# One dense tile's gates from one-hots, two tiles' gates added into a zeroed array, selection per head

## The chip, the cores and the metric

The kernel runs on one core of one Trainium2 chip. The metric is device time in microseconds, the median of several runs. TensorE (PE) does the matmuls, VectorE (DVE) the elementwise work, the top-16 and the selection, ScalarE (ACT) copies, gelu and exponentials and issues some DMAs, GpSimd (POOL) a few elementwise operations and all indirect DMAs, and SyncE (SP) issues the plain loads. PEld is TensorE's loading of weights, which overlaps its matmuls.

## What is computed

A decoder trunk of two layers over 512 tokens and 16 meta tokens, width 1024. Layer 0 mixes tokens by pooling, layer 1 by a stick-breaking attention; after each comes a PEER block, an expert layer of 128 x 128 = 16384 experts, which is where nearly all of the time goes:

```python
def chunk(hx):                                            # h: (tokens, 1024)
    q = einsum('btd,dq->btq', hx, w_query)                # 8 heads x 2 halves x 128
    s = einsum('bthpc,hpnc->bthpn', q, sub_keys)          # 128 keys for each half
    top_s, top_i = lax.top_k(s, 16)
    cand_s = top_s[..., 0, :, None] + top_s[..., 1, None, :]
    cand_i = top_i[..., 0, :, None] * 128 + top_i[..., 1, None, :]
    best_s, best_pos = lax.top_k(cand_s, 16)              # of the 256 sums
    expert = take_along_axis(cand_i, best_pos)
    gate = softmax(best_s)
    act = gelu(einsum('btd,bthkd->bthk', hx, u[expert]))
    return einsum('bthk,bthkd->btd', gate * act, v[expert])
```

So every token takes 8 x 16 = 128 experts, each with a gate.

## The kernel before

The 512 tokens are four tiles of 128. PEER treats them in two ways. Tile 3 (`GATHERED`) and the meta tokens are gathered: for each of the 128 slots of a token, POOL fetches that expert's 8 KB row of u and v by an indirect DMA (L343, 128 rows at once, one for each partition), DVE forms the dot product with the token (L355), ACT the gelu, and DVE adds the gated v half to the output (L367). A row is four quarter-steps of `row_step()`: fetch, dot, gelu, add. Tiles 0 to 2 are dense: all 16384 experts are computed for their 384 tokens. The experts come as 128 blocks j of 128. A u step (`u_parts`, L307) loads the block's u, splits it in a high and a low part (`w_hi` on ACT, L279; `w_lo` = `w` - `w_hi`, L281 on DVE or L283 on POOL), does 24 matmuls into `psu` (L314), a gelu on ACT and writes the activation `ac` to DRAM (`aout`). A v step (`v_step`, L660) loads v (L663), the activations (L668) and, for each four blocks, the gates (`gt`, L672), splits v (`v_hi` on ACT, `v_lo` on DVE, L676), multiplies activations by gates (`wt`, L678), splits that (`wt_hi` on ACT, L682; `wt_lo` on DVE, L683) and does 18 matmuls into six PSUM banks `y` (L690), which gather over all 128 blocks.

The gates of the dense tiles, zero for all but 128 of a token's 16384 experts, are made by one-hots (`build_gates`, L553): for four tokens at a time DVE makes three one-hot tiles `ab`, PE multiplies them (8 matmuls into `pg`, L574 and L576, one block), ACT evacuates that to `stage` (L581) and sends a stage of 32 tokens to the DRAM array `gout` (L584). That is 32 blocks a tile, 96 a layer.

A layer's PEER block runs in three stages:

- Stage A: for each of 8 heads, two query projections (weights split as those of u), scores, and on DVE the top-16 of both halves of all four tiles (`top16`, L391). For the gathered tile the selection (`select`, L399: 80 candidate sums, their top-16, the look-up of the experts' two indices by one-hots at L439 to L445, the softmax) follows per head, and its rows are queued. u steps are put between as a plan says: `WQ_DVE` and `WQ_PE` are its costs of a head in us, a u step is put in while PE's sum lies below DVE's. Here `w_lo` is made on POOL.
- Stage B: per dense tile one selection over all 8 heads (128 slots a partition), then its 32 gate blocks. `gate_stream` yields a cost at each step and quarters of u steps are put between by it; rows are worked off at a pace of `ROW_PERIOD`. The order on PE is kept as written (`pin`), `w_lo` is made on DVE.
- Stage C: the u steps that are left alternate with v steps, then v steps alone; rows go on at their pace. Nothing of the next layer starts before its end.

All indirect DMAs are on POOL's queue q0. Loads of w, v, `ac` and `gt` are issued by SP, in the order written, and `aout` and `gout` writes by ACT. Layer 0's PEER is preceded by the pool mixer (0 to 55 us), layer 1's by the attention (1399 to 1795 us).

## Time and profile before

| | |
|---|---|
| Median of 3 runs | 3134.08 us (3131.5 to 3134.3) |
| The profiled execution | 3127.99 us, its span 3126.3 us |
| Mean granted PE clock | 0.984 of 2.4 GHz |
| PE, PEld busy | 2999.0 us (96%), 2671.7 us (85%) |
| DVE, ACT, POOL busy | 2449.1 us (78%), 1354.3 us (43%), 688.7 us (22%) |
| DMA moved | 758.52 MB, 243 GB/s on the mean |

Busy is the time in which an engine had an instruction running. A matmul's end is modelled, so several can overlap in the records, and prices of PE are best read from one start to another. The span is cut by hand into stages; layer 0's A, B and C begin at 55.5, 264 and 650.4 us, layer 1's at 1795, 2010 and 2391.3 us. DMA share is the mean busy share of 16 DMA engines; a packet is one piece of a transfer, by one descriptor.

### The profile page before, as it was taken

Reading aid. Unit: us, or ns where it says so; the run is one execution under the profiler, and the core shown is the slowest. Engines: PE = TensorE matmul, PEld = TensorE weight load, DVE = VectorE, ACT = ScalarE, POOL = GpSimd, SP = SyncE. Lnnn points to the kernel's source line nnn. Section 1 sums busy time; section 2 is a strip of 40 time slices with the busy share of each in tenths; the row PEclk is TensorE's granted clock in tenths of the full one; section 3 lists DMA queues with packets and bytes.
Section 4 is the critical chain, followed back from the end, with each engine's and each line's share of the span. In section 5 each row is a group of like instructions: output and inputs, shape, how many; then the busy total and the mean of one; then the engine's idle time right before and its main releaser. Section 6 shows DMA issues by size and latency. Waiting matters only on the chain.

```text
span 3126.3 us, 45813 instructions
## 1 busy us (share of the span) xinstructions
PE 2999.0 (96%) x16514; PEld 2671.7 (85%) x16514; DVE 2449.1 (78%) x5636; ACT 1354.3 (43%) x2184; POOL 688.7 (22%) x704
## 2 busy tenths in 40 slices
PE   8988999999999999999999989799999999999999
PEld 7887988988888888879965778798898888888887
DVE  3999998878777778786456469999987777777765
ACT  3443645643333333335455334354655333333333
POOL 3431311111111111114245244222110111111100
PEclk9999999999999999999999999999999999999999
DMA  3435877799989899762100344477878998989875
GB/s 134 179 121 202 282 265 265 274 360 329 338 312 321 314 329 329 273 245 90 55 1 1 108 177 144 158 262 269 303 253 326 358 314 321 331 308 333 307 250 164
DMA packets 286708, 758.52 MB, mean 243 GB/s; under 512 B 23184, under 2 KB 176784, under 8 KB 248336
## 3 DMA queue, kind: packets, MB, share of 16 engines
q1 hardware_dynamic: 222544, 390.92, 36.8%
q0 software_dynamic: 39168, 285.23, 24.9%
q10 hardware_dynamic: 24768, 79.44, 6.6%
q8 instruction: 129, 2.11, 0.3%
q14 instruction: 99, 0.81, 0.1%
HBM read 673.99 MB, written 81.53 MB: 242 GB/s over the span
## 4 chain that ended last, share of the span: by engine, by line
PE 77%; DVE 16%; DMA 3%; ACT 2%; issue 1%; POOL 0%; SPq 0%; DVEq 0%; ACTq 0%; POOLq 0%
PE y L690 31%; PE psu L314 27%; PE pg L574 3%; PE pg L576 3%; PE pp L124 2%; PE pp L125 2%; PE pp L123 2%; DVE mr L395 1%; DVE prod L355 1%; DVE w_lo L281 1%; DMA gt<-gout 1%; DVE ti L397 1%; DVE hx L367 1%; DMA w<-in_peer_ut_dram 1%; DVE ti L394 1%
## 5 line engine op out<-in xcount | busy, mean ns | idle before, releaser
L343 POOL DMA_INDIRECT row<-in_peer_uv_dram,ei x272 | 383.3, 1409 | 1833.1 <-DVE hx L367 1481.9
L314 PE MATMUL psu<-n_hi,w_lo 128*128 128x384 f32 x2048 | 701.5, 343 | 42.4 <-DVE w_lo L281 39.9
L314 PE MATMUL psu<-n_hi,w_hi 128*128 128x384 f32 x2048 | 720.4, 352 | 11.5 <-ACT ac L321 7.2
L314 PE MATMUL psu<-n_lo,w_hi 128*128 128x384 f32 x2048 | 703.0, 343 | 0.6 <-DVE n_lo L118 0.6
L279 ACT ACTIVATE w_hi<-w 128x1024 fp32r<-128x1024 f32 x288 | 305.6, 1062 | 467.7 <-PE psu L314 373.2
L690 PE MATMUL y<-v_lo,wt_hi 128*128 128x512 f32 x1536 | 473.6, 390 | 1.6 <-DVE v_lo L676 1.6
L690 PE MATMUL y<-v_hi,wt_hi 128*128 128x512 f32 x1536 | 473.8, 390 | 0.5 <-ACT v_hi L675 0.5
L690 PE MATMUL y<-v_hi,wt_lo 128*128 128x512 f32 x1536 | 473.6, 389 | 0.0
L314 PEld LDWEIGHTS psu<-n_hi,w_lo 128*128 128x128 f32 x2048 | 394.0, 192 | 49.0 <-DVE w_lo L281 45.8
L314 PEld LDWEIGHTS psu<-n_hi,w_hi 128*128 128x128 f32 x2048 | 395.4, 193 | 17.8 <-ACT ac L321 7.5
L314 PEld LDWEIGHTS psu<-n_lo,w_hi 128*128 128x128 f32 x2048 | 394.0, 192 | 5.5 <-DVE n_lo L118 1.1
L682 ACT ACTIVATE wt_hi<-wt 128x384 fp32r<-128x384 f32 x256 | 134.3, 525 | 574.0 <-PE y L690 295.5
L683 DVE TENSOR_TENSOR wt_lo<-wt,wt_hi 128x384 fp32r<-128x384 f32 x256 | 142.5, 557 | 264.3 <-ACT wt_hi L682 264.3
L281 DVE TENSOR_TENSOR w_lo<-w,w_hi 128x1024 fp32r<-128x1024 f32 x228 | 278.2, 1221 | 83.2 <-ACT w_hi L279 82.6
L690 PEld LDWEIGHTS y<-v_lo,wt_hi 128*128 128x128 f32 x1536 | 288.1, 188 | 63.3 <-DVE v_lo L676 2.9
L690 PEld LDWEIGHTS y<-v_hi,wt_lo 128*128 128x128 f32 x1536 | 288.3, 188 | 60.4
L355 DVE SCALAR_TENSOR_TENSOR prod<-row,hnat 128x1024 bf16<-128x1024 f32 x272 | 337.7, 1241 | 0.6 <-DMA row<-in_peer_uv_dram,ei 0.5
L367 DVE SCALAR_TENSOR_TENSOR hx<-row,gwt,hx 128x1024 f32<-128x1024 f32 x256 | 334.5, 1307 | 2.1
L690 PEld LDWEIGHTS y<-v_hi,wt_hi 128*128 128x128 f32 x1536 | 286.8, 188 | 52.8 <-ACT v_hi L675 0.9
L676 DVE TENSOR_TENSOR v_lo<-v,v_hi 128x1024 fp32r<-128x1024 f32 x256 | 312.2, 1219 | 5.4 <-ACT v_hi L675 5.2
L581 ACT ACTIVATE stage<-pg 128x512 f32<-128x512 f32 x192 | 216.9, 1137 | 149.2 <-PE pg L576 146.3
L675 ACT ACTIVATE v_hi<-v 128x1024 fp32r<-128x1024 f32 x256 | 270.8, 1058 | 10.6 <-DMA v<-in_peer_uv_dram 9.5
(313 smaller groups left out, 4695.0 us busy)
## 6 DMA issues: line engine op xcount, KB each, us to landing
w<-in_peer_ut_dram SPq DMA_DIRECT2D x256, 512.0 KB, 5.9
v<-in_peer_uv_dram SPq DMA_DIRECT2D x256, 512.0 KB, 6.1
gout<-stage ACTq DMA_DIRECT2D x24, 2048.0 KB, 8.4
gt<-gout SPq DMA_DIRECT2D x64, 768.0 KB, 10.2
aout<-ac ACTq DMA_DIRECT2D x148, 192.0 KB, 4.0
ac<-aout SPq DMA_DIRECT2D x148, 192.0 KB, 5.9
w<-in_peer_wq_dram SPq DMA_DIRECT2D x32, 512.0 KB, 3.4
wn<-in_w_kv_dram SPq DMA_DIRECT2D x8, 1024.0 KB, 5.5
```

The lines of the kernel that those rows point to most:

```text
L279: amark.append(sc.activation(whi, w, AF.Copy))
L281: vmark.append(v.tensor_sub(wlo, w, whi.bitcast(F32)))
L314: m = pin(pe.matmul(ps[:, :ND], a[:, k, :], b[:, k, c0:c0 + ND], start=st, stop=en))
L343: gp.indirect_dma_start(out=row, out_offset=None, in_=peer_uv, in_offset=bass.IndirectOffsetOnAxis(ap=item[1], axis=0))
L355: v.scalar_tensor_tensor(prod, row[:, :D], 1.0, hn_nat[i], ALU.mult, ALU.mult, accum_out=dot)
L367: v.scalar_tensor_tensor(acc, row[:, D:], wt, acc, ALU.mult, ALU.add)
L581: sc.activation(stage[:, :, o:o + TG].rearrange("p j t -> p t j"), pg, AF.Copy, scale=1.0 / GSCALE)
L675: amark.append(sc.activation(vhi, v32, AF.Copy))
L676: vmark.append(v.tensor_sub(vlo, v32, vhi.bitcast(F32)))
L682: sc.activation(whi, wt, AF.Copy)
L683: vmark.append(v.tensor_sub(wlo, wt, whi.bitcast(F32)))
L690: pe.matmul(y[n][half], wp[:, ts], vq[:, half * 512:(half + 1) * 512], start=st, stop=en)
```

## The change

Gates. Only tile 0's gates are still built from one-hots (`BUILT` = 1: 32 blocks a layer), in an array of their own, `gbuilt`. For tiles 1 and 2 the array `gout` is cleared, and each gate is added to its element there: `gates_out` works out the element's index for each slot, and `scatter` issues an indirect DMA with an addition for one slot of 128 tokens, 4 bytes for each partition, 2 tiles x 16 slots x 8 heads = 256 a layer. Each waits for the same tile's scatters of the head before (or for the clearing): two heads of a token may choose the same expert. The clearing is four DMAs a layer on ACT's queue from a zero tile, for layer 0 within the pool mixer, for layer 1 at the start of attention.

Selection. `select` runs once a head over all four tiles (64 slots a partition, 16 for each tile) in stage A, for the dense tiles too; stage B has none.

Pace. `w_lo` is always made on DVE. With `WQ_DVE` 33 and `WQ_PE` 15.5 / 14.5 the plan puts 38 u steps (layer 0) and 40 (layer 1) into stage A. There each head issues 17 scatters and eight quarter-steps of rows (two rows). Stage B runs u steps up to `EARLY` = 118, one gate block beside each of the first u steps, the scatters left spread evenly over them, and rows at `ROW_PERIOD`. PE's order is no longer pinned. In stage C ten u steps are left beside 128 v steps. `gt` is read in two parts; the second waits for the last head's scatters.

```diff
+BUILT = 1
...
-ROW_PERIOD = ((18.0, 13.5), (18.0, 13.5))
-WQ_DVE = (19.0, 19.0)
-WQ_PE = (15.5, 12.5)
+ROW_PERIOD = (12.0, 13.5)
+ROWS_A = 2
+WQ_DVE = 33.0
+WQ_PE = (15.5, 14.5)
 GATHERED = (3,)
 LEAD = (2, 2)
-QUIET = 16
+EARLY = 118
+SCATTER_A = 17
...
+    zero = const([P, 512], F32, "zero")
+    gp.memset(zero, 0.0)
...
+    NB = P // TB
+    NS = nd - BUILT
+    gbuilt = [dram.tile([P, BUILT * NB, NK, TB], F32, name=f"gbuilt{layer}") for layer in range(2)]
+    gouts = [dram.tile([P * NS * NB * NK * TB, 1], F32, name=f"gout{layer}") for layer in range(2)]
+    cleared = [[], []]
+    def clear_gates(layer, part, parts):
+        g = gouts[layer].rearrange("(p c f) o -> p c (f o)", p=P, f=512)
+        n = NK * NS * P // 512 // parts
+        cleared[layer].append(sc.dma_start(g[:, part * n:(part + 1) * n, :],
+                                           zero.unsqueeze(1).to_broadcast([P, n, 512])))
...
             pre(0)
+            clear_gates(0, 0, 4)
             fold()
             for i in range(1, NT):
                 pre(i)
+                clear_gates(0, i, 4)
...
-                if gating[0]:
-                    vmark.append(v.tensor_sub(wlo, w, whi.bitcast(F32)))
-                else:
-                    gp.tensor_sub(wlo, w, whi.bitcast(F32))
+                vmark.append(v.tensor_sub(wlo, w, whi.bitcast(F32)))
...
+            to_scatter = []
+            placed = {}
+            issued = []
+            def gates_out(h, i1, i2, gate):
+                ds = slice(BUILT * TK, nd * TK)
+                ef = gr.tile([P, NS, TK], F32, name="gf", bufs=2)
+                at = gr.tile([P, NS * TK], I32, name=f"at{h}")
+                v.scalar_tensor_tensor(ef, i1[:, ds].rearrange("p (n q) -> p n q", q=TK), float(TB),
+                                       tok[:, :NS].unsqueeze(2).to_broadcast([P, NS, TK]), ALU.mult, ALU.add)
+                v.scalar_tensor_tensor(at, i2[:, ds], float(NS * NB * NK * TB), ef.rearrange("p n q -> p (n q)"),
+                                       ALU.mult, ALU.add)
+                to_scatter.extend((h, n, at[:, n * TK + q:n * TK + q + 1],
+                                   gate[:, (BUILT + n) * TK + q:(BUILT + n) * TK + q + 1])
+                                  for n in range(NS) for q in range(TK))
+            def after(x, y, sync=True):
+                kind = mybir.DependencyClass.Sync if sync else mybir.DependencyClass.NoSync
+                tc.add_manual_dep(x.ins, y.ins.name, mybir.DependencyInfo(kind, mybir.DependencyReason.DATA),
+                                  reason="gates")
+            def scatter(count):
+                for _ in range(min(count, len(to_scatter))):
+                    h, n, at, gate = to_scatter.pop(0)
+                    x = gp.indirect_dma_start(out=gout, out_offset=bass.IndirectOffsetOnAxis(ap=at, axis=0),
+                                              in_=gate, in_offset=None, compute_op=ALU.add)
+                    if issued:
+                        after(x, issued[0], sync=False)
+                    issued.append(x)
+                    earlier = placed[n, h - 1] if h else cleared[layer]
+                    for e in earlier:
+                        after(x, e)
+                    tc.declare_no_dep(x.ins, group=f"gates{layer}", keep=[e.ins for e in earlier],
+                                      reason="one head's slots of a token are distinct experts")
+                    tc.add_to_no_dep_group(f"gates{layer}", x.ins)
+                    placed.setdefault((n, h), []).append(x)
             def gather_rows(i, h, i1, i2, gate, ns, acc, first):
                 ef = gr.tile([P, TK], F32, name="ef", bufs=2)
@@ -340,8 +395,11 @@
                 def fetch():
                     item = todo.pop(0)
                     row = gr.tile([P, 2 * D], F32, name="row", bufs=NROW)
-                    gp.indirect_dma_start(out=row, out_offset=None, in_=peer_uv,
-                                          in_offset=bass.IndirectOffsetOnAxis(ap=item[1], axis=0))
+                    x = gp.indirect_dma_start(out=row, out_offset=None, in_=peer_uv,
+                                              in_offset=bass.IndirectOffsetOnAxis(ap=item[1], axis=0))
+                    for y in issued:
+                        after(x, y, sync=False)
+                    issued[:] = [x]
...
-                        td += WQ_DVE[layer]
+                        td += WQ_DVE
                         tu += WQ_PE[layer]
...
+                        i1, i2, gate = select(qp, gr, f"h{h}", tv, ti, NT)
+                        gates_out(h, i1, i2, gate)
+                        for dst, src in zip(picked, (i1, i2, gate)):
+                            v.tensor_copy(dst[:, :, h * TK:(h + 1) * TK],
+                                          src[:, :BUILT * TK].rearrange("p (n q) -> p n q", q=TK))
+                        scatter(SCATTER_A)
+                        for _ in range(4 * ROWS_A):
+                            row_step()
                         for i in gathered:
-                            res = []
-                            for _ in select(qp, gr, f"g{i}_{h}", tv[i][:, h:h + 1], ti[i][:, h:h + 1], 1, res):
-                                pass
-                            gather_rows(i, h, *res, TK, hx[i], False)
-                        while tr < tq and row_step():
-                            tr += ROW_PERIOD[layer][0] / 8
+                            of = slice(i * TK, (i + 1) * TK)
+                            gather_rows(i, h, i1[:, of], i2[:, of], gate[:, of], TK, hx[i], False)
...
-                            sc.dma_start(gout[:, n * (P // TB) + tb], stage)
+                            sc.dma_start(gbuilt[layer][:, n * NB + tb], stage)
...
+                left = len(to_scatter)
+                first = j0
+                blocks = gate_stream()
                 tu = tr = 0.0
+                n = 0
+                while j0 < EARLY:
+                    for _ in u_parts(j0, True, ("u", j0 + 1)):
+                        n += 1
+                        if n % 3 == 0:
+                            next(blocks, None)
+                    j0 += 1
+                    scatter(left * (j0 - first) // (EARLY - first) - (left - len(to_scatter)))
+                    tu += ucost
+                    while tr < tu and row_step():
+                        tr += ROW_PERIOD[layer] / 8
+                for _ in blocks:
+                    pass
+                scatter(len(to_scatter))
...
+                        gts[jg] = vp.tile([P, nd * NB, JG, TB], F32, name="gt", bufs=3)
+                        js = slice(jg * JG, (jg + 1) * JG)
+                        sy.dma_start(gts[jg][:, :BUILT * NB], gbuilt[layer][:, :, js, :])
+                        x = sy.dma_start(gts[jg][:, BUILT * NB:], gates[:, :, js, :])
+                        for n in range(NS):
+                            for e in placed[n, H - 1]:
+                                after(x, e)
...
+                    for part in range(4):
+                        clear_gates(1, part, 4)
```

## Rows read from the trace of the kernel before

**Rows 1.** Busy by stage: window, length, PE, PEld, DVE, ACT, POOL, clock, DMA, GB/s

```profile
55.50:264.00 208.50, 180.29 (x1254) 175.56 (x1255) 183.70 (x922) 83.48 (x148) 76.28 (x40) 0.94 0.42 149
264.00:650.40 386.40, 365.32 (x2268) 344.70 (x2267) 350.32 (x864) 209.78 (x271) 77.95 (x31) 0.98 0.75 268
650.40:1385.00 734.60, 733.14 (x3510) 643.74 (x3509) 583.89 (x841) 278.38 (x457) 112.79 (x100) 1.00 0.90 323
1795.00:2010.00 215.00, 191.60 (x964) 170.34 (x963) 180.96 (x871) 86.53 (x122) 91.52 (x46) 0.96 0.43 152
2010.00:2391.30 381.30, 359.22 (x2237) 339.19 (x2235) 346.38 (x849) 204.97 (x264) 65.72 (x31) 0.98 0.76 271
2391.30:3126.30 735.00, 729.73 (x3475) 638.37 (x3474) 554.51 (x792) 273.38 (x440) 96.04 (x85) 1.00 0.86 302
```

**Rows 2.** PE timeline (start, us, engine, line, tile), layer 0, stage A, 33 rows

```profile
58.75 0.33 PE L314 MATMUL psu<-n_hi,w_hi 128*128 128x384 f32 x1
...
64.37 0.34 PE L314 MATMUL psu<-n_hi,w_lo 128*128 128x384 f32 x1
```

**Rows 3.** PE timeline around a gate block of eight matmuls

```profile
320.88 0.29 PE L574 MATMUL pg<-ab 128*128 128x128 f16 x1
...
322.02 0.34 PE L314 MATMUL psu<-n_lo,w_hi 128*128 128x384 f32 x1
```

**Rows 4.** DVE timeline, two v steps of layer 1 with no other work

```profile
3040.28 0.56 DVE L683 TENSOR_TENSOR wt_lo<-wt,wt_hi 128x384 fp32r<-128x384 f32 x1 [1.79 <-ACT wt_hi L682]
...
3041.35 1.22 DVE L676 TENSOR_TENSOR v_lo<-v,v_hi 128x1024 fp32r<-128x1024 f32 x1
...
3044.36 0.56 DVE L683 TENSOR_TENSOR wt_lo<-wt,wt_hi 128x384 fp32r<-128x384 f32 x1 [1.79 <-ACT wt_hi L682]
```

**Rows 5.** DVE timeline, top-16 of 128 and of 80

```profile
144.83 0.48 DVE L393 MAX8 tv<-s 128x8 f32<-128x128 f32 x2
...
153.73 2.29 DVE L408 TENSOR_TENSOR cand<-tv 128x16 f32<-128x16 f32 x2
...
273.89 0.23 DVE L393 MAX8 bv<-cand 128x8 f32<-128x80 f32 x1
274.04 0.22 DVE L396 MAX8 bv<-mr 128x8 f32<-128x80 f32 x1
```

**Rows 6.** DVE timeline, look-up of one index for 128 slots

```profile
283.75 2.27 DVE L439 TENSOR_TENSOR oh<-iota_b,da 128x2048 bf16<-128x2048 bf16 x1
...
286.15 1.21 DVE L442 TENSOR_TENSOR oh<-oh,tib 128x2048 bf16<-128x2048 bf16 x1
...
287.43 2.27 DVE L445 TENSOR_REDUCE gdi<-oh 128x128 f32<-128x2048 bf16 x1
```

**Rows 7.** Costliest groups of the page: the two vector operations of a row

```profile
L355 DVE SCALAR_TENSOR_TENSOR prod<-row,hnat 128x1024 bf16<-128x1024 f32 x272 | 337.7, 1241 | 0.6 <-DMA row<-in_peer_uv_dram,ei 0.5
...
L367 DVE SCALAR_TENSOR_TENSOR hx<-row,gwt,hx 128x1024 f32<-128x1024 f32 x256 | 334.5, 1307 | 2.1
```

**Rows 8.** Stage A of layer 0, L314 alone, columns as in rows 1

```profile
55.50:264.00 208.50, 63.99 (x318) 58.23 (x319) 0.94 0.42 149
```

**Rows 9.** L343 alone: POOL's time in A and B, and the landing

```profile
55.50:264.00 208.50, 15.45 (x13) 0.94 0.42 149
264.00:650.40 386.40, 77.95 (x31) 0.98 0.75 268
...
DMA to landing us min/median/max: 5.4/8.6/15.6
```

**Rows 10.** DMA queues, packets, MB, share: 16.0 to 16.5 us; then whole span

```profile
q1 hardware_dynamic: 862, 0.02, 102.6%
...
q0 software_dynamic: 39168, 285.23, 24.9%
```

**Rows 11.** SP's own queue, issue of a weight load in stage C

```profile
685.71 7.98 SPq L276 DMA_DIRECT2D w<-in_peer_ut_dram  x1
```

**Rows 12.** 80 us of stage C, columns as in rows 1

```profile
640.00:720.00 80.00, 78.98 (x388) 70.51 (x389) 67.38 (x96) 32.13 (x54) 15.14 (x12) 1.00 1.03 384
```

More of the change, by code (lines that the diff above doesn't have):

```diff
@@ L84, in trunk_kernel @@
     sy.dma_start(hx[0], x[0, :P, :])
+    dense = [i for i in range(NT) if i not in GATHERED]
+    nd = len(dense)
+    assert dense == list(range(nd))
+    ND = nd * P
+    NB = P // TB
[8 more added lines that the diff above has]
+                                           zero.unsqueeze(1).to_broadcast([P, n, 512])))
     n_hi = const([P, KC, S + NM], F32R, "n_hi")
@@ L139, in pool_mixer @@
             v.tensor_copy(iota_x, iota_f.unsqueeze(2).to_broadcast([P, P, TG]))
+            blk = s1.tile([P, 1], I32, name="blk")
+            v.tensor_scalar(blk, pi, TB.bit_length() - 1, None, ALU.logical_shift_right)
+            at0 = s1.tile([P, 2], F32, name="at0")
+            v.tensor_copy(at0[:, 0:1], blk)
+            v.tensor_copy(at0[:, 1:2], pi)
+            v.scalar_tensor_tensor(tok[:, 0:1], at0[:, 0:1], float(NK * TB - TB), at0[:, 1:2], ALU.mult, ALU.add)
+            for n in range(1, NS):
+                v.tensor_scalar(tok[:, n:n + 1], tok[:, 0:1], float(n * NB * NK * TB), None, ALU.add)
             v.tensor_copy(iota_b, iota_f[:, :TK])
@@ L256, in peer @@
         gathered = list(GATHERED)
-        dense = [i for i in range(NT) if i not in gathered]
-        nd = len(dense)
-        c0 = dense[0] * P
-        assert dense == list(range(dense[0], dense[0] + nd))
-        ND = nd * P
-        NB = ND // TB
-        gout = dram.tile([P, NB, NK, TB], F32, name=f"gout{layer}")
+        gout = gouts[layer]
         aout = [dram.tile([P, ND], F32, name=f"aout{layer}_{j}") for j in range(NK)]
@@ L313, in u_parts @@
                                          (wlo, hi, False, k == KC - 1)):
-                        m = pin(pe.matmul(ps[:, :ND], a[:, k, :], b[:, k, c0:c0 + ND], start=st, stop=en))
+                        m = pe.matmul(ps[:, :ND], a[:, k, :], b[:, k, :ND], start=st, stop=en)
                         n += 1
@@ L384, in peer @@
                 ps1 = c1.enter_context(tc.tile_pool(name="ps1", bufs=2, reuse_waits="tile", space=PSUM))
-                tv = [tp.tile([P, H, 2, TK], F32, name=f"tv{i}") for i in range(NT)]
-                ti = [tp.tile([P, H, 2, TK], U32, name=f"ti{i}") for i in range(NT)]
                 if with_meta:
@@ L458, in select @@
                                     sm.unsqueeze(2).to_broadcast([P, nh, TK]), ALU.mult)
-                    res.append(gate)
-                    yield 1.0
+                    return (*res, gate)
+                picked = [gr.tile([P, BUILT, H * TK], F32, name=f"picked{q}") for q in range(3)]
                 ucost = 0.0098 * ND + 0.15
-                tq = tr = td = tu = 0.0
+                td = tu = 0.0
                 j0 = 0
@@ L599, in build_gates @@
                             place(*waiting.pop(0))
-                        yield 1.34
+                        yield
                     for wq in waiting:
                         place(*wq)
-                blocks = [nd * (P // TG)]
                 def gate_stream():
-                    if with_meta:
-                        res = []
-                        yield from select(gb, gr, "gm", tvm, tim, 1, res)
-                        gather_rows(NT, 0, *res, TK, ym, True)
-                    for n, i in enumerate(dense):
-                        res = []
-                        yield from select(gb, gb, "gd", tv[i], ti[i], H, res)
-                        for cost in build_gates(n, *res):
-                            blocks[0] -= 1
-                            yield cost
@@ L618, in peer @@
-                pcost = [0.0]
-                tu = tr = 0.0
-                td = 0.0
-                pinned[0] = gating[0] = True
-                steps = None
-                for cost in gate_stream():
-                    td += cost * DVE_SLACK
-                    tu += pcost[0]
-                    pcost[0] = 0.0
-                    while tu < td and (steps or j0 < NK):
-                        if steps is None:
-                            steps = u_parts(j0, True, ("u", j0 + 1) if j0 + 1 < NK else None)
-                            j0 += 1
-                        tu += ucost / UPARTS
-                        if next(steps, True):
-                            steps = None
-                    while tr < td and blocks[0] >= QUIET and row_step():
-                        tr += ROW_PERIOD[layer][0] / 8
-                        td += 4.7 / 8
@@ L638, in peer @@
-                if steps:
-                    drained(steps)
+                    for n in range(BUILT):
+                        yield from build_gates(n, *(t[:, n, :] for t in picked))
+                left = len(to_scatter)
+                first = j0
+                blocks = gate_stream()
+                tu = tr = 0.0
+                n = 0
[9 more added lines that the diff above has]
+                        tr += ROW_PERIOD[layer] / 8
```

50 lines of the change are left out of this document (20 added, 30 removed).

## The prediction

> **What bounds the kernel now.** Two views of the page come first: the share of each engine (PE leads) and the chain of waits (mostly PE, then DVE). They are means over unlike stages, so I read the busy times of each stage next, then PE's, DVE's and POOL's instructions in a stretch of each, and the queues last. In a stage, look for an engine whose busy time is the stage's length, and at the granted clock. A layer's PEER block has three stages: A (queries, scores, top-16), B (u matmuls beside the building of gates) and C (v matmuls beside the rest of u). In C, PE is busy 733 of 735 us and 730 of 735 us: C is as long as its matmuls. In A and B it is not: idle are 28.2 + 21.1 us in layer 0 and 23.4 + 22.1 us in layer 1, and the granted clock averages 0.94 to 0.98, which costs (1 - clock) x length = 12.5 + 7.7 + 8.6 + 7.6 us [rows 1]. Lost on PE in A and B together: 95 + 36 = 131 us. DVE is the reason: 183.7 busy of 208.5 us in A. So the time is PE's work plus what PE loses in A and B, and a change is worth what it does to these two.
>
> PE's prices come from start to start, since its busy times are modelled. A u step is 24 matmuls; 32 steps of the pipeline take 64.37 - 58.75 = 5.62 us, 0.176 us each, so 4.22 us [rows 2]. A gate block (8 matmuls for 4 tokens) pushes the next u matmul but one from 320.88 to 322.02, less its own 0.18: 0.97 us [rows 3]. A v step alone comes every 4.08 us [rows 4].
>
> **Part 1: gate blocks removed.** Of 3 x 32 blocks a layer 64 go, 128 in all: 128 x 0.97 = 124 us of PE work that nothing hides. With them go 128 x 4 one-hot operations on DVE and 128 evacuations on ACT, both off the path.
>
> **Part 2: A and B after.** Selection runs once per head over four tiles (64 slots a partition). DVE per head: eight top-16 sets of 128 wide, 9.4 us (8.9 us lie between the starts shown, the last set's tail follows); four sets of 80, six operations each at 0.15 from start to start, 3.6 [rows 5]; index look-up for 64 slots, half of what 128 slots take, (2.27 + 1.21 + 2.27) for each of two indices / 2 = 5.75 [rows 6]; some 25 short operations at 0.15, 3.7. That is 22.5. Residuals w_lo, which leave POOL for DVE, have v_lo's shape and operation, 1.22 busy, 1.14 from start to start [rows 4]: two for queries and 4.7 for u steps, 7.6. Two rows at 2.5 (1.24 + 1.31, overlapping a little) [rows 7], 5. Sum 35 us. PE per head: A now holds 318 u matmuls (56 us) in 180.3 - 12.5 us at full clock [rows 1, 8], so 112 / 8 = 14 us, and with 4.5 u steps 33. DVE begins some 20 us after PE and is 2 us a head slower: PE waits some 25 us a layer, with a slower clock 30. By the plan's rule A covers 38 u steps in layer 0 and 40 in layer 1. In B a u step, with one block 4.22 + 0.97 = 5.19 us, stands against 1.14 for w_lo, some 1.4 for one-hots and 2.5 / 1.5 = 1.6 for rows, 4.2 us of DVE; the dense tiles' selections, which B has now, are gone. I take 8 us a layer for B. So 131 lost becomes 76: 55 saved. Bounds of the new loss: 20 (PE runs ahead into B's u steps) to 131 (nothing gained). POOL no longer reads both halves of a weight beside DVE; the 2.29 us of two tiny additions at 153.73 are what such a meeting may look like [rows 5].
>
> **Part 3: scatters.** 256 a layer, each 128 elements of 4 bytes, added in DRAM. On POOL an indirect DMA costs 15.45 / 13 = 1.19 us in A and 77.95 / 31 = 2.51 in B [rows 9]. A: 17 scatters and 2 rows a head, 19 x 1.19 = 23 of 35 us. B: 120 scatters and 52 (layer 1: 45) rows; while blocks run (32 u steps, 166 us) 48 + 21 of them at 2.51 take 173 us, just beyond, and in the 203 us afterwards there is room. The one-hots are two-input f16 operations on DVE, and the trace has 2.51 where they run against 1.19 where they don't. The Trainium skill (SBUF — State Buffer, "SBUF: two separate sides") says that DVE can lock GpSimd out while it writes descriptors; the trace agrees so far, and by that rule alone the sum would stay, as the rows hold it already. Queued behind a late scatter are row gathers, and DVE waits for those. I take 0, up to 20 us a layer.
>
> On the queue, the unknown is a packet's price p. Eight packets fall to each of 16 engines. Near by size: 859 plain 4-byte reads in 0.5 us of 16 engines, 0.01 us [rows 10]. Near by queue and issuer: rows, 39168 packets in 24.9% of 16 x 3126 us, 0.318 us for 8 KB [rows 10]. An accumulate reads and writes, so some multiple of 0.01; it is nearer to that row, as bytes hardly count. Where does p begin to cost? A: 17 x 8p + 2 x 8 x 0.318 = 35 at p = 0.22; B: 120 x 8p + 52 x 2.54 = 369 at p = 0.25. Below about 0.23 the queue keeps up and I take 0.
>
> Waits: each scatter waits for the 16 of the head before in its tile; at least 16 others lie between, 19 us of issue. The first gate read on SP waits for the last head's scatters, with v and w loads queued behind it; three u steps (12.7 us) cover the usual landing of 8.6 [rows 9].
>
> **Part 4: clearing.** 2 x 16.8 MB of zeros go from ACT's queue in pieces of 2 KB, four DMAs of 2048 pieces a layer, early in the pool mixer and at the start of attention. DMA engines have room there; ACT may not. An issue can hold its engine when much is queued: 7.98 us on SP for a load behind gate reads [rows 11]. At 384 GB/s [rows 12] a quarter drains in 10.9 us. Low: 0. High: parts 2 to 4 hold ACT 33 us in each layer, with every copy and exponential queued behind: 65. I take 35, since most issues in the trace are short but these are the largest. The zero tile and its POOL memset: 2.
>
> **Part 5: C.** All but 10 u steps now lie ahead of C, so v steps follow each other at 4.08 us, each with a load of 0.52 MB, 0.20 of activations, 0.20 of gates, and a row of 1.05 MB each 1.53 steps (layer 1: 1.73). While rows last (10 u and 109 v steps, 487 us) layer 0 moves 5 + 57 + 19 + 22 + 82 = 185 MB, 380 GB/s, and layer 1 176 MB, 361. C now moves 323 and 302 at a share of 0.90 and 0.86, so 359 and 351 if full [rows 1]: by that 29 + 14 = 43 us longer. But 80 us at 384 GB/s cost PE 1 us [rows 12]. I take 28, bounds 0 and 43. DVE: v 1.22 + 0.56 + 0.56 (wt has the shape of wt_lo), rows 2.7 / 1.53, 0.92 for overlap: 3.8 of 4.08 us, close but inside.
>
> **The sum.** -124 - 131 + 76 + 35 + 2 + 28 = -114. The profiled execution took 3128.0 us (span 3126.3): 3014. Its median of three lies 6 us higher (3134.1), so I say **3020**.
>
> **Rivals.**
> First, the covers hold: clearing and C cost nothing, 3020 - 63 = 2957. For it: 384 GB/s without loss, and empty DMA engines in attention. Against: the held issues.
> Second, the covers fail: ACT is held for the full 65, C takes 43, POOL lags 20 a layer: 3020 + 30 + 15 + 40 = 3105.
> Third, slower: the scatters' queue ends last. Place: q0, shared with the row gathers; POOL waits for scatters of the head before, rows behind it come late, DVE waits for rows and PE for DVE. Price: 2 x 256 x 8 x (p - 0.23) = 4096 x (p - 0.23) us, which eats the 114 from p = 0.26 on. At a row packet's 0.318 it is 360 us: 3380. For it: that price is in the trace on this queue. Against: 0.01 for small reads.
> Fourth, accumulates don't overlap at all: a scatter lasts at least the shortest landing of an indirect DMA, 5.4 us [rows 9]. A: 8 x (17 x 5.4 - 35 + 5) = 495, B: 120 x 5.4 + 132 - 369 = 410, both layers + 1800: 4820. The Trainium skill (DMA: Bandwidth & Descriptors, "Latency and other measured facts") has some 0.8 us for the shortest round trip to HBM; eight in a row would make an estimate of 6.4 us a scatter and some 5200 us. No run shows accumulates; small reads in the trace overlap.
> Fifth, it moves work and PE's losses stay at 131 while C and clearing cost their upper ends: 3020 + 55 + 30 + 15 = 3120, within what can't be told or nearly.
>
> **How the numbers follow.** Forecast 0.42, first rival 0.16, second 0.14, third 0.22, fourth 0.03, fifth 0.03. A measurement of this kernel tells 0.2%, 6 us, from no change. Faster: 0.42 + 0.16 + 0.11 = 0.69 (a fifth of the second rival reaches the old time); same 0.03; slower 0.28. The likeliest case alone runs from 2950 to 3100. The range takes in the first rival with 30 us below it, the second, and the third up to p = 0.275: 2925 to 3200; outside lie most of the third and the fourth.
>
> **What would show it.** L690 and psu matmuls of B back to back, with idle PE in A of 20 to 40 us a layer: part 2. 64 pg blocks left: part 1. Landing of scatters under 20 us, and DVE never waiting long for `row`: part 3; a landing that grows from head to head, and PE waiting behind `prod`, is the third rival. ACT's DMA issues of some 10 us ahead of the pooled copies or the first exponentials: part 4. C longer than 564 us by more than 30: part 5. I am wrong first of all if 4-byte accumulates cost above 0.23 us a packet, or if the longer v-only stretch finds DMA or DVE short.

## The result: 132 us slower, in the stages that were to become shorter

The changed kernel takes 3265.77 us (median of 4 runs, 3265.46 to 3267.32) where the kernel before takes 3134.11: a ratio of 1.0423, 95% interval 1.0405 to 1.0441. The prediction was 3020 us, with a range from 2925 to 3200.

The times at which the first u matmul, the first v matmul and the last v matmul of a layer start divide the span, for both kernels alike:

| us | before | after | difference |
|---|---|---|---|
| pool mixer, to the first u matmul | 55.5 | 87.9 | +32.4 |
| A and B, layer 0 | 598.1 | 822.2 | +224.1 |
| C, layer 0 | 745.0 | 559.1 | -185.9 |
| attention, to the first u matmul | 395.4 | 426.6 | +31.2 |
| A and B, layer 1 | 600.5 | 811.0 | +210.5 |
| C, layer 1 | 726.6 | 552.2 | -174.4 |

The six differences add up to 137.9 us; the span grew by 137.8 (3264.1 against 3126.3). Stage C gave what was expected of it: u steps left it, and nearly nothing came in their place. Ahead of the first v matmul stand 122 u steps a layer in the changed kernel (four of the ten that the plan leaves for C among them), 76 and 80 in the kernel before. So A and B took 46 and 42 u steps (some 194 and 177 us), lost 64 gate blocks (62 us a layer) and, with the 55 us saved that part 2 forecast, should have grown by some 105 and 90 us; they grew by 224 and 211.

The page of the changed kernel: busy time, granted clock in 40 slices, queues, and the clearing's row of the DMA issues.

```profile
PE 2931.5 (90%) x15478; PEld 2600.8 (80%) x15478; DVE 2293.1 (70%) x5087; ACT 1196.2 (37%) x2030; POOL 1386.7 (42%) x1157
PEclk9979899999999999999989997999899999999999
q1 hardware_dynamic: 236240, 408.23, 37.4%
q0 software_dynamic: 112896, 285.52, 28.7%
q10 hardware_dynamic: 51648, 96.75, 8.0%
gout<-zero ACTq DMA_DIRECT2D x8, 4096.0 KB, 26.5
```

PE has less to do than before and is busy 90% of a longer span. POOL's busy time has doubled. The clock row shows dips at 7 and 8 in both layers' stage A, where [rows 1] has 0.94 and 0.96.

Busy times by stage as in [rows 1]: A, B and C of layer 0, then of layer 1.

```profile
87.90:488.00 400.10, 308.51 (x1879) 297.54 (x1879) 284.50 (x1190) 122.70 (x204) 257.46 (x158) 0.88 0.53 134
488.00:897.00 409.00, 385.31 (x2196) 375.75 (x2196) 282.47 (x462) 156.08 (x250) 295.48 (x172) 0.96 0.96 314
897.00:1469.00 572.00, 564.51 (x2494) 466.23 (x2495) 474.86 (x702) 219.42 (x353) 82.77 (x78) 0.99 0.93 335
1895.70:2303.00 407.30, 309.40 (x1519) 276.80 (x1520) 287.52 (x1178) 122.52 (x176) 250.33 (x157) 0.88 0.53 133
2303.00:2694.00 391.00, 371.58 (x2118) 362.24 (x2117) 256.52 (x392) 150.09 (x235) 274.76 (x165) 0.96 0.96 304
2694.00:3264.00 570.00, 562.05 (x2522) 470.08 (x2520) 456.93 (x667) 213.20 (x339) 69.14 (x65) 1.00 0.91 324
```

Stage A lasts 400 us and 407 us, and no engine fills it: PE 77%, DVE 71%, POOL 64%, at a clock of 0.88. In B it is PE again that is busiest, with 24 and 19 us idle. So the question is first what the engines wait for in A.

### The profile page after: what moved, and what is told of

The parts are those of the page before. It is cut to its first block, busy times and chain, and to the rows that moved or that the text cites. A ratio compares the mean times of both kernels' runs of the same rounds, so it can differ in the third digit from the quotient of the medians.

```text
span 3264.1 us, 43981 instructions
## 1 busy us (share of the span) xinstructions
PE 2931.5 (90%) x15478; PEld 2600.8 (80%) x15478; DVE 2293.1 (70%) x5087; ACT 1196.2 (37%) x2030; POOL 1386.7 (42%) x1157
## 3 DMA queue, kind: packets, MB, share of 16 engines
q0 software_dynamic: 112896, 285.52, 28.7%
## 4 chain that ended last, share of the span: by engine, by line
PE 62%; DVE 15%; DMA 10%; POOL 5%; issue 4%; ACT 2%; ACTq 1%; SPq 0%; DVEq 0%; POOLq 0%
PE y L738 24%; PE psu L331 20%; POOL gout L371 5%; DMA v<-in_peer_uv_dram 4%; DMA ac<-aout 2%; DVE w_lo L306 2%; PE pp L146 2%; PE pp L147 2%; PE pp L145 2%; DVE prod L413 1%; DVE mr L451 1%; DVE hx L425 1%; PE psu L560 1%; PE psq L561 1%; ACTq L105 1%
## 5 line engine op out<-in xcount | busy, mean ns | idle before, releaser
L331 PE MATMUL psu<-n_hi,w_lo 128*128 128x384 f32 x2048 | 711.0, 348 | 114.3 <-DVE w_lo L306 114.3
L398 POOL DMA_INDIRECT row<-in_peer_uv_dram,ei x272 | 333.0, 1224 | 1055.8 <-DVE hx L425 848.6
L331 PE MATMUL psu<-n_lo,w_hi 128*128 128x384 f32 x2048 | 712.4, 348 | 0.6 <-DVE n_lo L140 0.6
L306 DVE TENSOR_TENSOR w_lo<-w,w_hi 128x1024 fp32r<-128x1024 f32 x288 | 352.2, 1223 | 325.8 <-ACT w_hi L305 324.5
L331 PEld LDWEIGHTS psu<-n_hi,w_lo 128*128 128x128 f32 x2048 | 400.6, 196 | 125.9 <-DVE w_lo L306 125.6
L738 PEld LDWEIGHTS y<-v_lo,wt_hi 128*128 128x128 f32 x1536 | 286.2, 188 | 74.3 <-DVE v_lo L724 16.5
L726 DVE TENSOR_TENSOR wt<-ac,gt 128x384 f32<-128x384 f32 x256 | 141.9, 555 | 36.5 <-DMA gt<-gout 22.2
```

The costliest lines, as they stand in the source:

```text
L306: vmark.append(v.tensor_sub(wlo, w, whi.bitcast(F32)))
L331: m = pe.matmul(ps[:, :ND], a[:, k, :], b[:, k, :ND], start=st, stop=en)
L398: x = gp.indirect_dma_start(out=row, out_offset=None, in_=peer_uv, in_offset=bass.IndirectOffsetOnAxis(ap=item[1], axis=0))
L726: v.tensor_mul(wt.rearrange("p (b t) -> p b t", t=TB), ac.rearrange("p (b t) -> p b t", t=TB), gts[jg][:, :, j % JG, :])
L738: pe.matmul(y[n][half], wp[:, ts], vq[:, half * 512:(half + 1) * 512], start=st, stop=en)
```

## What the trace shows

**A head.** The starts of `gf` (one instruction a head, right in the selection) stand 26.7 us apart for the first two heads, then 95.1, then 43.5, 45.1, 43.5, 45.1 and 42.3 us (layer 1: 26.7, 99.6, then 43.6 to 44.6). The forecast had 35 throughout. One head on DVE's timeline (start, duration, line, tile, the idle time before it with its releaser) and the piece of PE's timeline that belongs to it:

```profile
320.14 0.49 DVE L449 MAX8 tv<-s 128x8 f32<-128x128 f32 x2 [0.60 <-ACT s L579]
...
351.14 1.22 DVE L413 SCALAR_TENSOR_TENSOR prod<-row,hnat 128x1024 bf16<-128x1024 f32 x1
...
353.61 1.21 DVE L306 TENSOR_TENSOR w_lo<-w,w_hi 128x1024 fp32r<-128x1024 f32 x1
...
354.83 1.21 DVE L306 TENSOR_TENSOR w_lo<-w,w_hi 128x1024 fp32r<-128x1024 f32 x1
...
364.81 0.49 DVE L449 MAX8 tv<-s 128x8 f32<-128x128 f32 x2 [0.67 <-ACT s L579]
```

```profile
354.88 0.53 PE L560 MATMUL psu<-n_hi,w_lo 128*128 128x264 f32 x1 [1.97 <-DVE w_lo L306]
355.43 0.42 PE L560 MATMUL psu<-n_hi,w_hi 128*128 128x264 f32 x1
...
361.74 0.28 PE L561 MATMUL psq<-n_hi,w_lo 128*128 128x264 f32 x1
```

DVE starts on a head's scores at 320.14, goes through top-16, selection and two rows, and at 353.61 and 354.83 makes the last two w_lo; the first of them is that of the next head's second query weight. Only with that can PE finish the second projection (354.88 to 362; L560 and L561 are its two halves of columns), then come the scores, and DVE begins its next head at 364.81. So nearly 35 us of DVE and 10 us in which it mostly waits for PE follow each other, though each engine has work for some 35 us only (DVE is busy 35.9 of these 44.7 us). The w_lo was not late for a load or a buffer, since ACT had made its w_hi by 344.98; it stood 8.6 us in DVE's queue, behind the look-up and the rows:

```profile
343.92 1.06 ACT L305 ACTIVATE w_hi<-w 128x1024 fp32r<-128x1024 f32 x1 [1.87 <-PE psu L331]
```

PE itself stood still for the second weight's w_lo for 2.0 or 5.8 us in a head of layer 0; the rest of the 9 us beyond its 35 are shorter waits and a lower clock (0.92 on the mean of these 44.7 us).

**The first rows.** POOL's timeline at the first scatters (the idle time before the first is the time since POOL's last work):

```profile
139.14 1.78 POOL L371 DMA_INDIRECT gout<-h0gate,at  x1 [48.74 <-DMA aout<-ac]
141.22 1.57 POOL L371 DMA_INDIRECT gout<-h0gate,at  x1 [0.30 <-issue]
143.10 1.55 POOL L371 DMA_INDIRECT gout<-h0gate,at  x1 [0.30 <-issue]
...
198.87 1.55 POOL L371 DMA_INDIRECT gout<-h0gate,at  x1 [0.30 <-issue]
200.73 1.55 POOL L371 DMA_INDIRECT gout<-h1gate,at  x1 [0.31 <-issue]
202.58 1.55 POOL L371 DMA_INDIRECT gout<-h1gate,at  x1 [0.30 <-issue]
204.43 1.01 POOL L398 DMA_INDIRECT row<-in_peer_uv_dram,ei  x1 [0.30 <-issue]
```

Most scatters start every 1.85 us, 1.55 busy and 0.30 between, even where DVE does nothing (from 173 us on). The first row fetch stands behind 34 of them, 65 us after the first, and DVE sits idle for 37.01 us until that row:

```profile
210.04 1.23 DVE L413 SCALAR_TENSOR_TENSOR prod<-row,hnat 128x1024 bf16<-128x1024 f32 x1 [37.01 <-DMA row<-in_peer_uv_dram,ei]
```

By groups, over the whole span (count, busy us, mean ns): scatters of the first and of the fifth head, and the row fetches.

```profile
L371 POOL DMA_INDIRECT gout<-h0gate,at x64 | 104.4, 1631 | 117.6 <-DMA aout<-ac 98.7 <-issue 18.9
L371 POOL DMA_INDIRECT gout<-h4gate,at x64 | 121.9, 1905 | 19.5 <-issue 19.5
L398 POOL DMA_INDIRECT row<-in_peer_uv_dram,ei x272 | 333.0, 1224 | 1055.8 <-DVE hx L425 848.6 <-DVE gwt L421 118.1 <-DVE gain L425 59.0
```

**The clearing.** ACT and its DMA queue (ACTq), layer 0 and then layer 1:

```profile
24.62 1.06 ACT L118 ACTIVATE junk<-hx 128x1024 bf16<-128x1024 f32 x1 [16.26 <-DMA hx<-in_x_dram]
...
31.22 13.91 ACTq L105 DMA_DIRECT2D gout<-zero  x1
...
45.17 1.09 ACT L255 ACTIVATE pooled<-pp 128x512 f32<-128x512 f32 x2 [12.86 <-issue]
...
1653.90 26.54 ACTq L105 DMA_DIRECT2D gout<-zero  x4
1680.47 1.28 ACT L915 ACT_TABLE_LOAD   x1 [26.20 <-issue]
```

In layer 0 the loads of tokens come late beside 16.8 MB of zeros (16.26 us of waiting at 24.62; the 16 DMA engines are busy from 5 to 55 us, at a share of 1.00 to 1.08 in each 5 us), and one issue holds ACT for 13.91 us. In layer 1 four issues in a row hold it for 26.54 us ahead of the first exponential.

## The experiments

Two theories of stage A were set against each other. Theory Q: the query chain just shown. Theory P: POOL's scatters with their waits. All kernels are the changed one with the edit named, but for b1; e3 and e11 leave the gates of tiles 1 and 2 out. e2, e3, e5 and e11 have one run each. "A" below runs from the first u matmul to the eighth selection, "B" from there to the first v matmul.

| | time, us | heads 4 to 8 apart, us | A, layers 0 / 1 | B, layers 0 / 1 |
|---|---|---|---|---|
| after | 3265.8 | 42 to 45 | 388 / 395 | 434 / 416 |
| e1 queries ahead | 3200.5 | 34 to 39 | 349 / 354 | 432 / 420 |
| e2 scatters in B | 3598.8 | 42 to 45 | 350 / 354 | 640 / 622 |
| e3 no scatters | 3165.2 | 42 to 45 | 349 / 354 | 422 / 412 |
| e4 clearing spread | 3232.9 | 42 to 45 | 392 / 395 | 427 / 414 |
| e5 query w_lo on POOL | 3255.2 | 34 to 50 | 382 / 392 | 430 / 416 |
| e6 rows first | 3238.2 | 42 to 45 | 355 / 364 | 447 / 436 |
| e7 = e1 + e4 + e6 | 3164.0 | 30 to 41 | 317 / 320 | 472 / 457 |
| e8 = e7, 14 in A | 3134.6 | 30 to 42 | 320 / 322 | 448 / 435 |
| e9 = e7, two built | 3170.7 | 30 to 42 | 313 / 324 | 474 / 456 |
| e10 = e8, 126 u steps | 3113.1 | 31 to 41 | 316 / 320 | 459 / 449 |
| e11 = e8, no scatters | 3062.6 | 32 to 42 | 317 / 321 | 415 / 399 |

**e1, the query weights ahead.**

```diff
+                        for kk in (("w", 2 * h + 2), ("w", 2 * h + 3)):
+                            if h + 1 < H and kk not in ahead:
+                                ahead[kk] = load_w(peer_wq[layer, kk[1]], qp)
                         i1, i2, gate = select(qp, gr, f"h{h}", tv, ti, NT)
```

The edit also gives these weights' w_hi and w_lo buffers of their own (`qp` above), so it changes two things at once; by the row at 343.92 it was the place in DVE's queue that held the w_lo, and buffers alone weren't tried.

> Edit: the next head's two query weights are loaded and split (w_hi, w_lo, in buffers of their own) ahead of this head's selection; before, the second one's w_lo stood behind selection and rows on DVE. Theory Q (the query chain): a head of stage A takes 44.3 us because DVE's 33 us (top-16, selection, two rows) and some 11 us (two w_lo, the second projection on PE, the scores) follow each other. With the chain opened a head falls to POOL's own 37 us (17 scatters from start to start 1.85 to 2.1, two rows 2.2): 8 heads x 2 layers x 7 = 112 us less, 3155. Theory P (POOL): a head is POOL's scatters with its waits for row buffers; the edit changes nothing there: 44 us a head, 3266 within 15.

3200.5 us, 1.0222 of the kernel before (1.0178 to 1.0266), 65 us less than the changed kernel. DVE's timeline, three heads:

```profile
292.63 0.16 DVE L357 SCALAR_TENSOR_TENSOR gf<-i,tok 128x32 f32<-128x32 f32 x1
...
328.30 0.16 DVE L357 SCALAR_TENSOR_TENSOR gf<-i,tok 128x32 f32<-128x32 f32 x1
...
367.50 0.16 DVE L357 SCALAR_TENSOR_TENSOR gf<-i,tok 128x32 f32<-128x32 f32 x1
```

35.7 and 39.2 us apart, where they were 45.1 and 43.5. The gain lies between the two theories' sums and is smaller than Q's: A is 39 and 41 us shorter, since only the later heads come closer; the third selection still starts 93 us after the second (102 in layer 1), as the first rows are still late.

**e2 and e3, where the scatters are.**

```diff
-SCATTER_A = 17
+SCATTER_A = 0
```

> Edit: no scatter is issued in stage A; all 256 of a layer are spread over the u steps of B. Theory Q: heads of A stay at 44 us, and only DVE's one wait of 37 us a layer for the first row goes; B becomes POOL's, 256 x 1.85 + 52 x 2.2 = 590 us where it had 410. Sum 3266 - 74 + 360 = 3550. Theory P: A's heads fall to DVE's 33 to 35 us as well, 150 us less than that: 3400.

```diff
-                    x = gp.indirect_dma_start(out=gout, out_offset=bass.IndirectOffsetOnAxis(ap=at, axis=0),
-                                              in_=gate, in_offset=None, compute_op=ALU.add)
+                    continue
```

> Edit: the scatters are not issued at all, so the gates of tiles 1 and 2 are left out (they stay zero); clearing, selection, rows and reads of gates are as in the changed kernel. Theory Q: heads of A stay at 44 us; the wait of 37 us a layer for the first row goes, and some 25 us a layer at the end of B: 3266 - 124 = 3140. Theory P: A's heads fall to 33 to 35 us, 16 x 10 = 160 us more: 2980.

3598.8 and 3165.2 us, 49 and 25 above theory Q's sums, 199 and 185 above theory P's. DVE's timeline of e3:

```profile
259.65 0.16 DVE L355 SCALAR_TENSOR_TENSOR gf<-i,tok 128x32 f32<-128x32 f32 x1
...
304.52 0.16 DVE L355 SCALAR_TENSOR_TENSOR gf<-i,tok 128x32 f32<-128x32 f32 x1
...
347.85 0.16 DVE L355 SCALAR_TENSOR_TENSOR gf<-i,tok 128x32 f32<-128x32 f32 x1
```

Without any scatter the heads stand 44.9 and 43.3 us apart, as with them; in e2 likewise. That settles theory P: POOL did not set the pitch of a head. What scatters did in A was the one late row: from the second to the third selection it takes 57 us in both, not 95. In B of e2 POOL has 256 scatters and 58 rows in 640 us: with 1.6 us for a row that leaves (640 - 93) / 256 = 2.1 us for a scatter, waits included.

**e4, the clearing spread.** Sixteen issues a layer, in layer 0 written four behind each tile's mixing, in layer 1 one at every third unit of the attention.

```diff
-            clear_gates(0, 0, 4)
...
+            for part in range(4):
+                clear_gates(0, part, 16)
             mixed(1, hx[1], 0)
...
-                    for part in range(4):
-                        clear_gates(1, part, 4)
...
+                            if n % 3 == 0 and n // 3 < 16:
+                                clear_gates(1, n // 3, 16)
```

> Edit: the clearing goes in 16 pieces a layer, in layer 0 behind the mixing of each tile (not among the first loads), in layer 1 spread over the attention's units. If what it cost was the first loads' wait for the DMA engines (the pool mixer ends 32 us later than before) and ACT held for 26.5 us by four issues at the start of attention, 32 + 13 to 26 us go: 3208 to 3221. If the 33.5 MB cost their time wherever they are put (or the first scatters now wait for them), the gain is under 15 us: 3250 or more.

3232.9 us (1.0325, 1.0257 to 1.0394), 33 less. The first u matmul starts at 71.2 instead of 87.9, and the attention takes 407.3 instead of 426.6: 16.7 and 19.3 us of the 63.6 us by which these two stretches had grown. In layer 0 the first pieces did not move as written: ACT still issues them at 1.49, 7.20 and 10.16 us, beside the loads of tokens, and waits for those nearly as long as before.

```profile
10.16 0.37 ACTq L105 DMA_DIRECT2D gout<-zero  x1
20.68 1.06 ACT L118 ACTIVATE junk<-hx 128x1024 bf16<-128x1024 f32 x1 [12.34 <-DMA hx<-in_x_dram]
```

In the attention some 8 of the 31.2 us were not the clearing's: b1 below, which clears nothing, takes 402.9 us there, against 395.4 in the kernel before.

**e5 and b1, the w_lo.** In e5 the flag `pool` is set for query weights.

```diff
-                vmark.append(v.tensor_sub(wlo, w, whi.bitcast(F32)))
+                if pool:
+                    gp.tensor_sub(wlo, w, whi.bitcast(F32))
+                else:
+                    vmark.append(v.tensor_sub(wlo, w, whi.bitcast(F32)))
```

> Edit: w_lo of the query weights is made on POOL again, as in the kernel before; that of u steps stays on DVE. Theory Q says that the query chain is what binds a head, wherever w_lo stands: on POOL it stands behind 17 scatters of 1.85 us, so a head stays at 44 us or becomes longer, up to 33 + 2 x 2.3 + 11 = 49: 3266 to 3340. Rival (DVE's work is what binds): two w_lo of 1.2 us leave DVE, a head falls by 2.4 us: 3228.

3255.2 us: 11 less, between the two expectations, by one run. Heads alternate between 42 and 46 us (one pair in layer 1 between 34 and 50). PE now waits for POOL:

```profile
298.15 0.59 PE L563 MATMUL psu<-n_hi,w_lo 128*128 128x264 f32 x1 [9.46 <-POOL w_lo L307]
```

That w_lo starts at 295.75 behind scatters and a row fetch, with its w_hi ready at 284.92. So it is not DVE as such that holds the chain: behind POOL's scatters the same step comes as late. And the same move in the kernel before, where selection of the dense tiles is not in the head:

```diff
-                if gating[0]:
+                if True:
```

> Edit, in the kernel before: w_lo in stage A is made on DVE instead of POOL, nothing else. Theory Q: the second projection of the next head then waits for DVE there too, so a head of A becomes longer by 3.4 x 1.2 = 4 us of DVE and by several us of exposed projection: 50 to 70 us a layer, 3230 to 3270. Rival: DVE's 25 us of idle time in A take it up: 3134 to 3155.

3143.5 us, 1.0034 (1.0021 to 1.0048): 9 us. The theory's 100 to 140 us were wrong here. Moving w_lo alone is nearly free; that it became the chain's link because at the same time each head's DVE work grew by a four-tile selection, which stands ahead of it, fits b1 and the rows above, but no run takes the selection alone.

**e6, the rows first.**

```diff
+                        for i in gathered:
+                            of = slice(i * TK, (i + 1) * TK)
+                            gather_rows(i, h, i1[:, of], i2[:, of], gate[:, of], TK, hx[i], False)
+                        for _ in range(4 * ROWS_A if h else NROW - 1):
+                            row_step()
                         gates_out(h, i1, i2, gate)
...
                         scatter(SCATTER_A)
-                        for _ in range(4 * ROWS_A):
-                            row_step()
```

> Edit: in each head of A the rows are queued and stepped ahead of the scatters (the first head only fetches three), where the first row fetch stood behind 34 scatters of 1.85 us. If that is why DVE waits 37 us for its first row and the third selection starts 95 us after the second, the interval falls to 44 to 57 us, as without any scatters: 38 to 50 us a layer, 3166 to 3190. If the wait is for something else (scores, weights), nothing changes: 3266.

3238.2 us (1.0335, 1.0313 to 1.0357), 28 less, where 76 to 100 were expected. The second and the third selection:

```profile
169.67 0.18 DVE L355 SCALAR_TENSOR_TENSOR gf<-i,tok 128x32 f32<-128x32 f32 x1
...
224.41 0.18 DVE L355 SCALAR_TENSOR_TENSOR gf<-i,tok 128x32 f32<-128x32 f32 x1
```

They stand 54.7 us apart (60.0 in layer 1), about as expected, and A is 33 and 31 us shorter; but B is 13 and 20 us longer. POOL has the same scatters to issue, and A now ends earlier.

**e7, these together.** e1, e4 and e6, and the last scatter eight u steps ahead of B's end.

> Edit: the query weights ahead (e1), the clearing spread (e4) and the rows first (e6) together, and the last scatter of B eight u steps earlier, so that the first read of gates doesn't wait for it. If the four costs are separate, their gains add up: 66 and 33 us as measured, 80 to 100 for the rows, 10 to 20 for the end of B: 3266 - 200 = 3050 to 3080, faster than the kernel before. If POOL binds as soon as DVE's chain is open (17 x 1.95 + 2 x 1.6 = 36 us a head), part of it goes: 3110.

3164.0 us, 1.0100 (1.0083 to 1.0117): 102 us less than the changed kernel, half of the 200 that the first sum promised (it counted 80 to 100 us for the rows, of which e6 alone gave 28). A is 71 and 75 us shorter than in the changed kernel, as much as e1 and e6 together (72 and 72), but B is 38 and 41 us longer. The border of A and B, in windows of 40 us, and what PE and DVE waited for from 385 to 500 us (total us, times, longest):

```profile
380.00:420.00 40.00, 30.65 (x152) 28.13 (x151) 37.10 (x116) 13.23 (x22) 33.90 (x21) 0.80 0.60 135
420.00:460.00 40.00, 20.44 (x119) 19.60 (x119) 14.46 (x29) 9.56 (x15) 33.91 (x21) 0.73 0.52 118
460.00:500.00 40.00, 24.08 (x121) 22.43 (x120) 21.70 (x43) 8.65 (x13) 32.52 (x21) 0.79 0.88 278
```

```profile
PE psu L338 <- DVE w_lo L311: 39.9, 5, 19.6
...
DVE prod L420 <- DMA row<-in_peer_uv_dram,ei: 35.6, 4, 22.2
```

POOL is busy 34 of 40 us, which with 0.30 us between 21 instructions is all of its time; at 395 us it issues scatters of the fourth head, when all eight have been selected. Row fetches stand behind these, DVE waits 35.6 us for rows, with w_lo queued behind, and PE 39.9 us for w_lo. With the chain open POOL is the bound, as theory P had it.

**e8 and e9, less for POOL.** e8 is e7 with fewer scatters in A, the last scatter six u steps ahead of B's end and a slower pace of rows in B; e9 is e7 with two tiles built from one-hots.

```diff
-SCATTER_A = 17
+SCATTER_A = 14
+ROW_B = (17.0, 19.0)
...
-                        tr += ROW_PERIOD[layer] / 8
+                        tr += ROW_B[layer] / 8
```

> Edit: e7 with 14 scatters a head in A instead of 17, the last scatter of B six u steps before its end, and a slower pace of rows in B (a row each 8.5 / 9.5 us of u work instead of 6 / 6.75), the rest of them in C. Theory P2 (POOL is the next bound): in e7 POOL enters B with scatters of four heads behind it, and rows stand behind these; PE loses some 50 us a layer at the border of A and B. With 14 x 1.95 + 2 x 1.6 = 31 us of POOL to a head of 35 it keeps up: 3164 - 100 = 3065, under the kernel before. Rival: B's loss is that of w and v loads (DMA share 0.9 to 1.0), which more rows in C make worse: 3164 to 3180.

```diff
-BUILT = 1
+BUILT = 2
-SCATTER_A = 17
+SCATTER_A = 8
```

> Edit: e7 with two tiles' gates built from one-hots (64 blocks a layer) and one tile's scattered (128 scatters a layer, 8 a head in A). Theory P2: POOL's need falls from some 600 to 350 us a layer, its backlog and the wait of the gate reads go (100 + 40 us), and PE does 64 blocks more, 64 x 0.97 = 62: 3164 - 140 + 62 = 3085. If scatters were no bound, only the blocks count: 3226.

e8 takes 3134.6 us, 1.0009 (0.9998 to 1.0020): level with the kernel before, and not 3065. The border is mostly mended (PE busy 35 and 36 of the 40 us from 420 and 460 on, where e7 has 20 and 24), but POOL is full up to the end of B, where PE stops:

```profile
720.00:760.00 40.00, 40.00 (x229) 40.00 (x228) 22.49 (x28) 13.53 (x22) 34.31 (x19) 1.00 0.90 270
760.00:800.00 40.00, 12.99 (x64) 12.28 (x63) 7.06 (x9) 4.90 (x9) 20.35 (x14) 0.66 0.70 191
```

```profile
DVE wt L738 <- DMA gt<-gout: 29.6, 1, 29.6
```

DVE waits 29.6 us for the gates of C, which wait for the last scatter (779.5 us). e9 takes 3170.7 us, 1.0111 (1.0091 to 1.0131), not 3085: 64 more blocks of PE work (62 us) just outweigh what 256 scatters less give.

**e10 and e11, how far it goes.**

```diff
-EARLY = 118
+EARLY = 126
```

> Edit: e8 with 126 u steps ahead of C instead of 118. In e8 POOL works without a gap (34 of each 40 us, the rest its own gaps between instructions) until 785 us, and PE waits some 27 us a layer at the end of B for the first gate read behind the last scatters. Theory P2: eight more u steps (34 us) fill that wait, and the end comes 2 x 25 us earlier: 3085, clearly under the kernel before. Rival: the waits move into C, whose v steps then have all loads to themselves (DMA share 1.03): 3120 to 3135.

> Edit: e8 without the scatters (gates of tiles 1 and 2 are left out, they stay zero). Gives what scatters cost in the mended kernel. Theory P2: the waits at the end of B go (2 x 27 us), and PE's losses at the border of A and B and in B, where rows stand behind scatters (2 x 20): 3134 - 94 = 3040. Rival: what is lost there is lost to the loads: only the 54 us go, 3080.

e10 takes 3113.1 us (3103.0 to 3128.8), a ratio of 0.9941 (0.9922 to 0.9960): faster than both kernels, by 0.6% against the one before, but nearer to the rival's 3120 than to 3085. The wait for the gates fell from 29.6 to 19.1 us only (25.4 to 13.1 in layer 1), since the last scatter came at 799.6 instead of 779.5 us:

```profile
DVE wt L738 <- DMA gt<-gout: 19.1, 1, 19.1
```

The rows that go with eight more u steps stand among the scatters, which may be why; it wasn't tried.

Without scatters (e11) the mended kernel takes 3062.6 us: 256 scatters a layer cost 72 us in all, 37 and 36 in A and B of the two layers. That lies between the two expectations.

## Why the prediction was wrong, by its own steps

**Part 2 failed, at the sum for a head.** The forecast put 35 us of DVE beside 33 us of PE and let them overlap, with PE waiting some 25 us a layer. DVE's 35 us were right (35.9 busy in a head). What was not asked is in which order the two engines need each other: a w_lo that the next projection needs was moved to DVE without looking at what would be queued ahead of it there (selection and rows). Measured are 44 us a head from the fourth on, and 92 and 98 us in which PE is idle in A, where 20 to 40 were the sign that part 2 holds. e1, which takes that w_lo out from behind the selection, gives 39 and 41 us in A back.

**Part 3 took the wrong row for POOL.** The forecast priced a scatter at 1.19 us, a row fetch's mean in stage A [rows 9], and got 23 us of POOL in a head. A scatter is 1.55 us or more and 0.30 us lie between instructions: in the head from 320.14 to 364.81 POOL is busy 31.45 us with 19 instructions, and with 19 gaps of 0.30 that is 37 us, more than DVE has. The gap is in no busy time, only in starts, and PE's prices were read from starts while POOL's were not. From it follow the first row behind 34 scatters (e6: 33 and 31 us in A) and, once A is short, a full POOL in B (e8 against e11: 37 and 36 us in A and B). The stated rule, that rows behind a late scatter make DVE wait, was right; "I take 0" was not, and its bound of 20 us a layer was too low for the first row alone.

PE's loss in A and B can be added up as in the forecast: 122 u steps ahead of the first v step x 4.22, 32 blocks x 0.97 and 112 us of queries make 658 us; 822 and 811 lasted, so 164 + 153 = 317 us were lost where 76 were forecast. (The same sum gives 130 for the kernel before, against the 131 read from its rows.) Of the 241 us between, e7 returns 67 (146 less in A, 79 more in B), e8 another 41 and e11 another 73. The last 60 also stand in e11, most of them in B (83 and 81 u steps with 32 blocks are 381 and 373 us, it has 415 and 399), and weren't taken apart.

**Part 4, the clearing**, was forecast at 35 + 2 us, and its two stretches grew by 32.4 + 31.2, some 8 of these by something else (b1). The hold of ACT was right for layer 1, 26.54 us by the row above against 33 as the upper bound. In layer 0 the place was wrong: "DMA engines have room there" overlooked the loads of tokens and weights, which keep the engines of the kernel before at a share of 0.99 and 1.02 from 5 to 10 and from 10 to 15 us and now share them with the zeros.

**Part 1 and part 5 were right or better.** 64 blocks are left. C takes 559 and 552 us; 6 u and 128 v steps alone would be 6 x 4.22 + 128 x 4.08 = 548, so 11 + 5 = 16 us are lost, where the kernel before lost 5 by the same sum: 11 us more and not 28.

**The rivals.** The third, which ends slower, had the right place (POOL's queue, rows behind scatters, DVE and PE behind these), but with the price on the DMA engines. q0 took 24.9% of 16 x 3126.3 us for 272 rows, and now 28.7% of 16 x 3264.1: by these rounded shares 2534 us more for 512 scatters, some 0.31 us on each engine for one. A scatter brings 144 packets (73,728 more on q0), so 0.034 us each, far from the 0.23 at which it would have counted. The price was in the issuing engine. Scatters land 2.9 to 10.9 us after their issue and start every 1.85 us, so they overlap, against the fourth rival. (Its second sum, at 6.4 us a scatter, comes to 5340 by its own steps and not 5200.) No rival had the query chain. While DVE is idle a scatter takes 1.54 to 1.57 us (90 of them); while it works most take as little, but some up to 2.63 and four in B from 3.01 to 4.40, with means of 1.63 for the first head and 1.91 for the fifth. The Trainium skill (SBUF — State Buffer, "SBUF: two separate sides") has DVE lock GpSimd out of writing descriptors; these times agree with a lock of small size, which no run sets apart from other causes.

The sum with measured terms: -124 - 131 + 317 + 64 + 11 = +137 us; measured were +138.

## What to carry to other kernels

When work is moved to another in-order engine, ask which instruction of the moved kind releases the next round elsewhere, and what will stand ahead of it; two engines with 35 us of work each can take 44 us a round. Price an issuing engine by starts, not by busy time, and multiply by the longest run of such instructions ahead of something urgent. When one bound is opened, a gain in its stage can be lost in the next: e7's A is 71 and 75 us shorter, the sum of what e1 and e6 gave there alone, but with POOL as the next bound B took 38 and 41 us of that back.

## What the hardware showed that was not expected

An indirect DMA that adds 128 elements of 4 bytes in DRAM costs little in the queue (0.31 us on each of 16 engines) and 1.85 us on POOL from start to start; a row fetch of 128 x 8 KB costs POOL less, 1.01 us (the median of 272; 1.47 on the mean in layer 0's stage A) and 0.30. One issue of 2048 pieces of 2 KB can hold ACT for 13.91 us, four in a row for 26.54. The granted clock fell to 0.88 on the mean of both stages A, where PE waits several times in each head: of 400 us that is 48, with 12.5 in the kernel before [rows 1].
